# Weight splits tied to earlier products, and their loads issued from ScalarE's queue, in the attention stage of a decoder step

## The chip, the core and the metric

The kernel runs on one core of a Trainium2 chip. The core has five engines, each with a queue of its own that it works through in order: TensorE (PE in the profile; PEld is its weight load), VectorE (DVE), ScalarE (ACT), GpSimd (POOL) and SyncE (SP, which here only issues DMAs). A DMA is issued by an instruction in one of these queues and then moved by the core's 16 DMA engines. Time is the device time of one execution in microseconds (us). A measurement consists of several executions of each kernel on the same chip; their median is given.

## The reference

One layer of a gated decoder for 1024 prompt tokens and 64 sample tokens (8 sequences of 8), all in float32:

```
u = rmsnorm(x);  [a | q | k | v | g_a | g_b] = u @ w_in
A: causal pooling of a over windows 2/4/8/16, a linear map per group, @ w_pa
B: QK-normed dilated sliding-window attention, 3 groups of 4 heads,
   (window, dilation) = (128,1), (512,4), (2048,16); groups combined
   by their softmax denominators, @ w_pb
h = x + (sigmoid(g_a) * A + sigmoid(g_b) * B) @ w_o
y = h + relu(rmsnorm(h) @ w_up)^2 @ w_down
```

It also returns the new key/value windows and the last rows of the pooling input.

## The kernel before

Every float32 product is made of three products of rounded parts: each operand is split into a rounded high part and a low rest. For weights this is done by `split` (lines 92 to 95): ScalarE writes the rounded copy (line 93), VectorE writes the difference (line 94). Weights come as panels of 256 columns. `panel` (line 102) takes a panel in four pieces of 512 columns of its layout, each holding two of the eight 128-row blocks: `raw_piece` (line 97) loads a piece of 256 KB into one of three buffers `raw` (the DMA is line 99), and `split` writes it to one of three places in the tile `places`, which successive panels use in turn. A buffer takes its next load when both halves of its last split are done.

The kernel first makes the pooling input `a`, then the attention's q, k and v (this stage, about 60 to 408 us), then the gates and branches, the output projection, and the two large products of the feed-forward part, which take about half of the time.

The attention stage runs over the head groups in the order g = 2, 1, 0. Each group has three panels, q (j = 0), k (j = 1) and v (j = 2), which fill all three places. So a panel of the next group overwrites the panel of the same kind of the group before, and its pieces cannot be written before the last product with that panel is done. A group runs through blocks of 128 tokens: block 8 (the 64 sample tokens) together with block 0, then 1 to 5, then 6 and 7 together (one after the other in group 0). For a pair of blocks the products go q, q, k, k, v, v; for single blocks q and k are one product. `qkv_part` (line 522) issues one such product and records its last matmul in `ends_of[g, blk, j]`; the squares, the norms, the scales and the copies out of PSUM follow on ScalarE, VectorE and GpSimd. Between the products come the steps of attention of blocks that are ready (scores `sg`, transposes `tpg`, outputs `pog`), of the pooling branch and of the sample attention, which reads its cached keys and values (`pck`, `pcv`, `kts`, `vts`).

Only TensorE's order is written out by hand, in program order. All other queues are ordered by the framework's planner, which simulates the program, takes earlier instructions first among those it holds ready, and may pull a load far ahead of its place. `behind_pe` (line 124) adds a dependency of an instruction on a matmul, which holds it back in that plan and on the chip. In `panel`, the argument `after` gives one such matmul to the copy (line 93) of each of the four pieces. `load` (line 959) is the local function that makes a panel of a group with a list of such matmuls; group 2's three panels have none.

In the before, all loads of these panels are issued from SP's queue, as are nearly all other DMAs of the stage: the stores of keys and values (line 929), of attention outputs (lines 705 and 708), the reads of cached keys and values (lines 730, 798, 846), and the moves of small tiles. Only the first three pieces of the very first panel (`a0`) are issued from ScalarE's queue.

Of the kernel before, what the change touches and what calls it, by code (L numbers as in the profile page):

```python
# [32 lines left out]
def decoder_step(ctx, tc, i, o):  # L33
    nc = tc.nc
    v_, s_, g_, t_ = nc.vector, nc.scalar, nc.gpsimd, nc.tensor
    dma = nc.sync.dma_start
# [7 lines left out]
    def rr(p, shape, dt, name, tag, bufs):  # L44

        n = turn[p, tag] = turn.get((p, tag), -1) + 1
        return p.tile(shape, dt, name=name, tag=f"{tag}.{n % bufs}", bufs=1)
# [44 lines left out]
    def split(dst_hi, dst_lo, src):  # L92
        ins = s_.activation(dst_hi, src, AF.Copy)  # L93
        v_.tensor_tensor(dst_lo, src, dst_hi.bitcast(F32), op=ALU.subtract)  # L94
        return ins

    def raw_piece(src, name, a, load=dma):
        raw = rr(wp, [P, 512], F32, name=f"raw_{name}_{a}", tag="raw", bufs=3)
        load(raw, src[:, a:a + 512])
        return raw  # L100

    def panel(src, name, between=None, after=None, ahead=None):

        n = src.shape[1]
        wt = places[:, place[0] % 3]
        place[0] += 1
        for a in range(0, n, 512):
            raw = ahead.pop(0) if ahead else raw_piece(src, name, a)
            if between is not None:
                between(a // 512)  # L110
            ins = split(wt[:, 0, a:a + 512], wt[:, 1, a:a + 512], raw)
            if after is not None:
                behind_pe(ins, after[a // 512])
        throttle.append(ins)
        return wt
# [38 lines left out]
    def bank(name):  # L154
        held[0] = (held[0] + 1) % 4
        return acc_p.tile([P, 512], F32, name=name, tag=f"acc.{held[0]}", bufs=1)
# [238 lines left out]
    def flush():  # L395
        while later:
            later.pop(0)()
# [113 lines left out]
    ends_of = {}  # L511
# [10 lines left out]
    def qkv_part(g, wts, blk, name, tiles, js):  # L522


        n = min(P, TOK - blk * P)
        qk, vt = tiles
        go = 0 if blk == 8 else g
        pt = bank(f"p{''.join('qkv'[j] for j in js)}{name}")
        js = sorted(js, key=lambda j: wts[j])
        N = 256 * len(js)  # L530
        at = places[:, wts[js[0]]:wts[js[-1]] + 1:max(1, wts[js[-1]] - wts[js[0]])]

        def rhs(s, k):
            return at[:, :, s, k * 256:(k + 1) * 256]

        if blk == 8:
            for k in range(KD):
                t_.matmul(pt[:, :N], smp_t[:, k, :], rhs(0, k), start=(k == 0), stop=(k == KD - 1))
                if k < KD - 1:
                    for kk in ((0, 1) if k == 0 else (k + 1,)):  # L540
                        last_mm[0] = t_.matmul(pt[:n, :N], smp_t[:, kk, :NS], rhs(1, kk), start=False, stop=False)
            v_.tensor_copy(vt[:n], pt[n:, :256])
            v_.tensor_tensor(pt[:n, :256], pt[:n, :256], vt[:n], op=ALU.add)
        else:
            gemm(pt[:n, :N], KD, lambda s, k: block_cols(g, blk, s, k), rhs, g == 0, step if N > 256 else None)
        for j in js:
            ends_of[g, blk, j] = last_mm[0]
        if blk < 8:
            if g == 0 and 2 in js and blk < 7:
                in_order(blk + 1)  # L550
        if js[0] < 2:
            ms = rr(ap1, [P, 8], F32, name=f"ms{name}_{js[0]}", tag="ms", bufs=4)
            r = rr(ap1, [P, 8], F32, name=f"mr{name}_{js[0]}", tag="mr", bufs=4)
            H = 4 * len(js)
            for u, j in enumerate(js):
                for h in range(4):
                    s_.activation(qk[:n, j * 256 + h * HD:j * 256 + (h + 1) * HD],
                                  pt[:n, u * 256 + h * HD:u * 256 + (h + 1) * HD], AF.Square,
                                  accum_out=ms[:n, 4 * u + h:4 * u + h + 1])
            v_.tensor_scalar(ms[:n, :H], ms[:n, :H], 1.0 / HD, xeps[go][:n, blk:blk + 1], op0=ALU.mult, op1=ALU.add)  # L560
            g_.tensor_tensor(r[:n, :H], ms[:n, :H], mhalf[:n, :H], op=ALU.pow)  # L561

            def scale():
                for u, j in enumerate(js):
                    for h in range(4):
                        behind_pe(s_.activation(qk[:n, j * 256 + h * HD:j * 256 + (h + 1) * HD],
                                                pt[:n, u * 256 + h * HD:u * 256 + (h + 1) * HD], AF.Copy,
                                                scale=r[:n, 4 * u + h:4 * u + h + 1]))
                    if j and blk == 8:
                        v_.tensor_tensor(qk[:n, 256:], qk[:n, 256:], wrow[:n], op=ALU.mult)  # L570
        else:
            s_.activation(vt[:n], pt[:n, :256], AF.Copy, scale=rtok[go][:n, blk:blk + 1])
        step()
        if js[0] < 2:
            soon(scale)
# [356 lines left out]
    for g in (2, 1, 0):  # L932
        nq = i["qk_norm"]
        if g == 1:
            assert ("p", 3) in done
            flush()
            pa.close()
            pam.close()
            ap2 = pb2.enter_context(tc.tile_pool(name="att2", bufs=1, reuse_waits="tile"))
            sp1 = psm.enter_context(tc.tile_pool(name="smp1", bufs=1, side="right", reuse_waits="tile"))  # L940
            np_ = psm2.enter_context(tc.tile_pool(name="nat", bufs=1, side="right", reuse_waits="tile"))
            sp = psm2.enter_context(tc.tile_pool(name="smp2", bufs=1, side="right", reuse_waits="tile"))
            osm = ap2.tile([P, 3, 4, 66], F32, name="osm")

            for a in range(2):
                v_.memset(osm[64:, a], 0.0)
                v_.memset(osm[64:, a, :, 64], -NEG)
            qs = sp1.tile([P, 768], F32, name="qs")
            for hf in range(2):
                dma(qs[64 * hf:64 * hf + 64], new_d[2].rearrange("t b c -> (t b) c"))  # L950
            wq = sp1.tile([P, 2, 256], F32, name="wq", tag="ss")[:, 0]
            dma(wq, bass.AP(tensor=nq.tensor, offset=nq.offset + 2 * 512, ap=[[0, P], [1, 256]]))
            v_.scalar_tensor_tensor(qs[:, :256], wq, HD ** -0.5, qs[:, :256], op0=ALU.mult, op1=ALU.mult)
            own_keys = sample_own_keys(qs)
        wrow = ap1.tile([P, 256], F32, name=f"wrow{g}", tag="wrow")
        dma(wrow, bass.AP(tensor=nq.tensor, offset=nq.offset + g * 512 + 256, ap=[[0, P], [1, 256]]))
        wts = [(place[0] + j) % 3 for j in range(3)]

        def load(j, *after):
            panel(i["w_in"][2 + 3 * j + g], f"qkv{g}_{j}", after=[ends_of[a] for a in after] or None)  # L960


        if g == 2:
            load(0)
            load(1)
            load(2)
        else:
            h = g + 1
            load(0, (h, 6, 1), (h, 7, 1), (h, 6, 2), (h, 6, 2))
            load(1, (h, 6, 2), (h, 7, 2), (h, 7, 2), (h, 7, 2))  # L970
        for blks in ((8, 0), (1,), (2,), (3,), (4,), (5,)) + (((6, 7),) if g else ((6,), (7,))):
            if g == 1 and 6 in blks:
                in_order(0)
            tiles = {b: qkv_tiles(f"{g}_{b}", b == 8) for b in blks}

            for js in (((0, 1), (2,)) if blks[0] in (1, 2, 3, 4, 5) else ((0,), (1,), (2,))):
                for b in blks:
                    qkv_part(g, wts, b, f"{g}_{b}", tiles[b], js)
                    if g < 2 and b < 8:
                        own_step(1)  # L980
                    if 2 in js:
                        (sample_block if b == 8 else prompt_block)(g, b, *tiles[b])
                if g == 2 and 2 in js and 8 in blks:
                    start(pool_branch(), "p", now=True)
                if g < 2 and 0 in js and 8 in blks:
                    load(2, (g, 8, 0), (g, 0, 0), (g, 0, 0), (g, 0, 0))


    while (2, "own") not in done:
# [68 lines left out]
    for d in range(4):  # L1058
# [6 lines left out]
        ahead = gate("b", d, *units[0], wgb, 3) if d else sgb0[0]  # L1065
        for u, (c, m) in enumerate(units):
# [3 lines left out]
            name = f"{d}_{c}_{m}"  # L1070
            ga, gb = sga[u], ahead
            if u + 1 < len(units):
                ahead = gate("b", d, *units[u + 1], wgb, 3) if d or u > 1 else sgb0[u + 1]
# [73 lines left out]
    for d in range(4):  # L1147
# [5 lines left out]
        for c0, n in CHUNKS if d < 3 else [(r * R4, R4) for r in range(4)]:  # L1153
            for m in range(2):
# [3 lines left out]
                for q in range(4):  # L1158
                    a, b = max(c0, q * R4), min(c0 + n, (q + 1) * R4)
# [462 lines left out]
    for g, rows in ((2, 60), (1, 63), (0, 60)):  # L1622
        src, dst = i[f"cache_kv{g + 1}"], o[f"kv{g + 1}_sample"]
# [107 lines left out]
```

## Time and profile before

| | us |
|---|---|
| median of 3 executions (lowest, highest) | 1478.26 (1478.07, 1479.83) |
| the profiled execution | 1477.96 |
| its span in the trace | 1476.2 |
| mean granted TensorE clock | 0.989 of full speed |
| attention stage, 60 to 408 us: TensorE busy | 334.55 of 348 |

The span runs from the first to the last instruction in the trace; what is around it belongs to the execution's time too. In the profile's rows a group is named by line, engine, operation and tiles (out<-in), with its count; a row of waits gives who waited for whom, the total, the number of times and the longest, in us. A row of a timeline gives the start, the duration and what ran; what stands in brackets is the idle time of the engine before it and what ended it. In a row of windows stand the stretch, its length, the busy time of each engine with its number of instructions, the granted clock of TensorE as a share of full speed, the share of the DMA engines that was busy, and the rate at which they moved data.

### The profile page before, as it was taken

The page shows a single profiled execution, that of the slowest core. Times are in us where ns is not written, and L with a number is a line of the kernel's source. Part 1 is how long each engine was busy: PE and PEld are TensorE (multiplying, and loading weights), DVE is VectorE, ACT ScalarE, POOL GpSimd, SP SyncE. Part 2 cuts the span into 40 slices and gives each one's busy share as a digit, 9 for nine tenths or more (in the row PEclk, how much of TensorE's full clock was granted, in tenths as well). Part 3 has the DMA queues.
Part 4 walks back from the last instruction along what each step waited for, and adds up shares of the span by engine and source line. Part 5 has one row for each costly group of instructions (what it writes and reads, how often), then busy time and mean ns, then how long its engine had stood idle before and what let it go on. Part 6 is the DMA issues. An engine that isn't in the chain of part 4 may idle for free.

```text
span 1476.2 us, 28005 instructions
## 1 busy us (share of the span) xinstructions
PE 1445.6 (98%) x10595; PEld 1397.7 (95%) x10595; DVE 996.5 (68%) x1949; ACT 687.3 (47%) x1885; POOL 395.8 (27%) x619
## 2 busy tenths in 40 slices
PE   8999899989999999999999999999999999999998
PEld 8988788878999999999998999999998999999998
DVE  7565555667864443434668998888988567666686
ACT  8466745567784222222445656566556322222220
POOL 1611236645400000010200221221125534343330
PEclk9999899999999999999999999999999999999999
DMA  6311656865446557479620776766677889787642
GB/s 219 97 47 64 195 140 168 216 181 122 119 119 206 193 183 258 148 216 301 251 101 16 274 286 252 273 237 261 255 273 290 321 298 327 258 294 261 238 186 112
DMA packets 124277, 304.72 MB, mean 206 GB/s; under 512 B 19111, under 2 KB 72045, under 8 KB 118830
## 3 DMA queue, kind: packets, MB, share of 16 engines
q1 hardware_dynamic: 101182, 187.81, 38.9%
q0 software_dynamic: 22528, 114.34, 21.9%
q8 instruction: 83, 1.36, 0.4%
q10 hardware_dynamic: 432, 0.79, 0.2%
q14 instruction: 52, 0.43, 0.1%
HBM read 218.49 MB, written 128.05 MB: 235 GB/s over the span
## 4 chain that ended last, share of the span: by engine, by line
PE 87%; DMA 4%; DVE 3%; issue 3%; ACT 1%; POOL 1%; SPq 1%; ACTq 0%; DVEq 0%; POOLq 0%
PE p1d L1202 13%; PE p1u L1202 11%; PE pga L136 6%; PE pgb L136 6%; PE p2d L1202 6%; PE p2u L1202 6%; PE ph L136 6%; PE pqk L136 5%; PE pv L136 4%; PE a L264 3%; PE pa L136 3%; PE p3d L1202 3%; PE p3u L1202 3%; PE pb L136 2%; DMA raw_qkv<-in_w_in_dram 1%
## 5 line engine op out<-in xcount | busy, mean ns | idle before, releaser
L1202 PE MATMUL p1d<-act,places 128*128 128x272 f32 x1104 | 191.2, 288 | 1.8 <-DVE places L94 1.1
L1202 PEld LDWEIGHTS p1d<-act,places 128*128 128x128 f32 x1104 | 163.2, 188 | 2.7 <-DVE places L94 1.3
L1335 POOL DMA_DIRECT2D z_d<-zs_M x105 | 56.2, 535 | 245.7 <-DVE zs_M L94 242.5
L1582 DVE TENSOR_TENSOR yd<-yd,p1d 128x544 f32<-128x544 f32 x116 | 83.0, 716 | 39.9 <-PE p1d L1202 39.9
L1629 POOL DMA_DIRECT2D out_kv_sample_dram<-in_cache_kv_dram x44 | 22.3, 508 | 310.5 <-ACT places L93 294.8
L1202 PE MATMUL p1u<-t,places 128*128 128x272 f32 x768 | 103.0, 291 | 0.7 <-ACT q L1449 0.7
L1202 PE MATMUL p1u<-act,places 128*128 128x272 f32 x768 | 102.2, 289 | 1.3 <-ACT q L1377 1.3
L93 ACT ACTIVATE places<-sd 128x512 fp32r<-128x512 f32 x64 | 37.4, 625 | 140.0 <-issue 108.0
L1202 PEld LDWEIGHTS p1u<-t,places 128*128 128x128 f32 x768 | 99.7, 191 | 0.8 <-ACT q L1449 0.8
L1202 PEld LDWEIGHTS p1u<-act,places 128*128 128x128 f32 x768 | 98.6, 188 | 1.8 <-ACT q L1377 1.5
L136 PE MATMUL pga<-act,places 128*128 128x384 f32 (+1 forms) x576 | 98.0, 328 | 0.0
L136 PE MATMUL pgb<-act,places 128*128 128x384 f32 (+1 forms) x576 | 97.8, 326 | 0.0
L1202 PE MATMUL p2d<-act,places 128*128 128x272 f32 x528 | 94.0, 288 | 1.6 <-DVE places L94 1.0
L136 PE MATMUL ph<-act,places 128*128 128x384 f32 (+2 forms) x624 | 95.4, 314 | 0.0
L136 PEld LDWEIGHTS pgb<-act,places 128*128 128x128 f32 x576 | 95.3, 188 | 0.0
L136 PEld LDWEIGHTS ph<-act,places 128*128 128x128 f32 x624 | 95.3, 188 | 0.0
L136 PEld LDWEIGHTS pga<-act,places 128*128 128x128 f32 x576 | 94.6, 188 | 0.3
L93 ACT ACTIVATE places<-rd 128x512 fp32r<-128x512 f32 x64 | 37.1, 625 | 94.7 <-PE p1d L1202 94.7
L1202 PEld LDWEIGHTS p2d<-act,places 128*128 128x128 f32 x528 | 78.9, 188 | 2.3 <-DVE places L94 1.2
L561 POOL TENSOR_TENSOR mr<-ms,mhalf 128x4 f32<-128x4 f32 (+2 forms) x39 | 49.7, 1273 | 112.9 <-DVE ms L560 107.4
L1534 POOL TENSOR_TENSOR sd<-rd 128x128 f32<-128x128 f32 x64 | 38.0, 594 | 118.6 <-DVE places L94 103.6
L94 DVE TENSOR_TENSOR zs_M<-q,zs_M 128x544 fp32r<-128x544 f32 x75 | 54.0, 722 | 18.8 <-ACT zs_M L93 18.8
(383 smaller groups left out, 3646.8 us busy)
## 6 DMA issues: line engine op xcount, KB each, us to landing
z_d<-zs_M POOLq DMA_DIRECT2D x105, 544.0 KB, 4.9
act<-z_d SPq DMA_DIRECT2D x73, 544.0 KB
out_kv_sample_dram<-in_cache_kv_dram POOLq DMA_DIRECT2D x36, 960.0 KB, 7.3
ru<-in_w_up_dram SPq DMA_DIRECT2D x16, 1024.0 KB
rd<-in_w_down_dram SPq DMA_DIRECT2D x15, 1024.0 KB
raw_qkv<-in_w_in_dram SPq DMA_DIRECT2D x36, 256.0 KB
zc<-z_d SPq DMA_DIRECT2D x16, 544.0 KB
pck<-in_cache_kv_dram SPq DMA_DIRECT2D x32, 256.0 KB
```

Of the source, the lines that this page charges most:

```text
L93: ins = s_.activation(dst_hi, src, AF.Copy)
L94: v_.tensor_tensor(dst_lo, src, dst_hi.bitcast(F32), op=ALU.subtract)
L136: last_mm[0] = t_.matmul(out, lhs(a, k), rhs(b, k), start=(j == 0), stop=(j == len(terms) - 1))
L264: last_mm[0] = t_.matmul(pts[m][:, :n], wt[:, a, kk, m * P:(m + 1) * P], act4[b][kk][:, :, part4(c)], start=(p == 0 and kk == 0), stop=(p ...
L561: g_.tensor_tensor(r[:n, :H], ms[:n, :H], mhalf[:n, :H], op=ALU.pow)
L1202: last_mm[0] = t_.matmul(pt[:, s, :R4], w(a, k), z(b, k, s), start=(start and j == 0), stop=(j == len(terms) - 1), skip_group_check=True)
L1335: g_.dma_start(z_d[f][AT[m]], st.rearrange("p b l -> p (b l)").bitcast(F32))
L1534: ins = g_.tensor_tensor(s[:, 0], a21, a22, op=ALU.add)
L1582: v_.tensor_tensor(part, part, p[src], op=ALU.add)
L1629: ins = g_.dma_start(d, a)
```

## The change

It has three parts, all for the panels of groups 1 and 0; group 2's stay as they are.

First, `panel` takes the issuing engine as an argument, and the 24 loads of groups 1 and 0 are issued from ScalarE's queue in place of SP's.

Second, the copies are tied to earlier products. Written as (product's block and kind), for the next group's pieces 1 to 4, with 6q for block 6 of the group before and s for the sample block of the group itself:

| panel | before | after |
|---|---|---|
| q | 6k, 7k, 6v, 6v | 7q, 6k, 6k, 7k |
| k | 6v, 7v, 7v, 7v | 7k, 6v, 6v, 7v |
| v | s q, 0q, 0q, 0q | 7v, s q, s q, s q |

Third, the v panel is made in the program one step earlier: right behind the sample's q product, where it stood behind block 0's q product.

```diff
-    def panel(src, name, between=None, after=None, ahead=None):
+    def panel(src, name, between=None, after=None, ahead=None, load=dma):
...
-            raw = ahead.pop(0) if ahead else raw_piece(src, name, a)
+            raw = ahead.pop(0) if ahead else raw_piece(src, name, a, load)
...
         def load(j, *after):
-            panel(i["w_in"][2 + 3 * j + g], f"qkv{g}_{j}", after=[ends_of[a] for a in after] or None)
+            panel(i["w_in"][2 + 3 * j + g], f"qkv{g}_{j}", after=[ends_of[a] for a in after] or None,
+                  load=nc.scalar.dma_start if after else dma)
...
-            load(0, (h, 6, 1), (h, 7, 1), (h, 6, 2), (h, 6, 2))
-            load(1, (h, 6, 2), (h, 7, 2), (h, 7, 2), (h, 7, 2))
+            load(0, (h, 7, 0), (h, 6, 1), (h, 6, 1), (h, 7, 1))
+            load(1, (h, 7, 1), (h, 6, 2), (h, 6, 2), (h, 7, 2))
...
                     qkv_part(g, wts, b, f"{g}_{b}", tiles[b], js)
+                    if g < 2 and b == 8 and 0 in js:
+                        load(2, (g + 1, 7, 2), (g, 8, 0), (g, 8, 0), (g, 8, 0))
...
-                if g < 2 and 0 in js and 8 in blks:
-                    load(2, (g, 8, 0), (g, 0, 0), (g, 0, 0), (g, 0, 0))
```

## The prediction, before the changed kernel was timed

> **What bounds it now.** First the page's head: the span, and how much of it TensorE (PE) works.
>
> ```profile
> span 1476.2 us, 28005 instructions
> PE 1445.6 (98%) x10595; PEld 1397.7 (95%) x10595; DVE 996.5 (68%) x1949; ACT 687.3 (47%) x1885; POOL 395.8 (27%) x619
> ```
>
> PE is the bound, 98% busy, so an edit of loads and waits can only win PE's pauses and the slow matmuls behind them. The waits of PE from 60 to 410 us, all attention, say who ends its pauses (total, times, longest):
>
> ```profile
> PE pv L541 <- DVE places L94: 4.9, 4, 3.1
> PE sg1b L597 <- ACT ocg1b L631: 2.5, 1, 2.5
> PE pq L541 <- DVE places L94: 2.0, 2, 1.3
> PE pv L538 <- ACT places L93: 1.9, 1, 1.9
> PE tps L828 <- DVE pxs L822: 0.9, 1, 0.9
> ```
>
> Three of the five name `places`, the split weights that the change is about. They sit at the two group changes: the v panel of group 1 (174 to 184 us), the q panel of group 0 (282 to 285 us). A pause costs more than itself. The windows just behind these pauses (length, PE busy, PEld, DVE, ACT, POOL, granted clock, DMA share, GB/s):
>
> ```profile
> 176.00:190.00 14.00, 9.13 (x42) 7.63 (x42) 5.84 (x19) 9.22 (x48) 3.93 (x5) 0.51 0.60 165
> 284.00:290.00 6.00, 5.40 (x43) 4.84 (x44) 3.80 (x8) 2.18 (x4) 2.82 (x4) 0.72 1.01 270
> 298.00:304.00 6.00, 5.08 (x30) 4.85 (x31) 4.26 (x17) 5.18 (x29) 1.53 (x3) 0.72 0.98 274
> ```
>
> The clock fell to 0.51, 0.72, 0.72 of full speed. Busy time at clock c loses (1 - c) of itself, so three places have a price:
>
> - A, group 1's v: pauses 1.9 + 4.9 = 6.8, plus 9.13 x 0.49 = 4.5: **11.3 us**.
> - B, group 0's q: pauses 2.0, plus 5.40 x 0.28 = 1.5: **3.5 us**.
> - C, the attention step sg1b: pause 2.5, plus 5.08 x 0.28 = 1.4: **3.9 us**.
>
> Together 18.7, with the 0.9 of tps 19.6 us: the most that the change can win.
>
> The Trainium skill, page "TensorE: Matmul & The Clock Gate", section "Part 1: The HAM clock gate", has the clock halved after an idle window of about 3.4 us. The floor of one half agrees with the 0.51; the pauses here are shorter each (3.1 us the longest) and still cost, so the rows decide. With the pauses alone the three places would hold 11.3 us, not 18.7.
>
> **Why A happens.** A piece of weights is loaded into one of three buffers, copied by ScalarE (ACT, L93), and the rest is subtracted by VectorE (DVE, L94); then the buffer takes the piece three places later. Group 1's first v piece follows the second k piece. Timelines of DVE, SP's queue and ACT:
>
> ```profile
> 162.91 0.69 DVE L94 TENSOR_TENSOR places<-raw_qkv,places 128x512 fp32r<-128x512 f32 x1
> ```
> ```profile
> 163.70 0.43 SPq L929 DMA_DIRECT2D out_kv_prompt_dram<-kw  x1
> 164.18 0.85 SPq L929 DMA_DIRECT2D out_kv_prompt_dram<-v  x1
> 165.07 1.12 SPq L950 DMA_DIRECT2D qs<-new_d  x2
> 166.28 0.53 SPq L952 DMA_DIRECT2D wq<-in_qk_norm_dram  x1
> 166.86 0.43 SPq L956 DMA_DIRECT2D wrow<-in_qk_norm_dram  x1
> 167.33 2.56 SPq L730 DMA_DIRECT2D pck<-in_cache_kv_dram  x2
> 169.99 2.41 SPq L99 DMA_DIRECT2D raw_qkv<-in_w_in_dram  x3
> ```
> ```profile
> 175.00 0.63 ACT L93 ACTIVATE places<-raw_qkv 128x512 fp32r<-128x512 f32 x1 [3.37 <-DMA raw_qkv<-in_w_in_dram]
> ```
>
> The buffer was free at 162.91 + 0.69 = 163.60; SP issued the load at 169.99, 6.4 us later, behind eight other DMAs; ACT had the data at 175.00 and a copy at 175.63, when PE had paused 1.9 us for it: PE wanted it from 173.7. The wait that ends last is thus SP's order, and then the transfer.
>
> **The ties.** The products that hold back the copies (b0 = block 0):
>
> ```profile
> 145.20 3.13 PE L136 MATMUL pk<-places,act 128*128 128x256 f32 x24
> 152.87 3.17 PE L136 MATMUL pv<-places,act 128*128 128x256 f32 x24
> 157.13 3.34 PE L136 MATMUL pv<-places,act 128*128 128x256 f32 x24
> 163.68 3.11 PE L136 MATMUL pq<-places,act 128*128 128x256 f32 x24
> ```
>
> They end at 148.3 (block 6's k), 156.0 and 160.5 (blocks 6's and 7's v), 166.8 (b0's q). The first copy moves from 148.3 to block 7's q, a product earlier. The second k piece, whose buffer the first v piece needs, moves from 160.5 to 156.0. The last three v pieces no longer wait for 166.8, but for the sample's q, done by 163.7.
>
> New chain at A: one load took 3.58 to 5.87 us from issue to landing (two rows of the chain of work), and ACT came to its first copy 1.9 us after its tie of 148.3:
>
> ```profile
> 158.65 3.58 DMA raw_qkv<-in_w_in_dram
> 176.76 5.87 DMA raw_qkv<-in_w_in_dram
> ```
> ```profile
> 150.22 0.70 ACT L93 ACTIVATE places<-raw_qkv 128x512 fp32r<-128x512 f32 x1
> ```
>
> The second k piece can be copied from 156.0. With 1.9 us for ACT to come to it and 0.63 + 0.69 for its two halves, its buffer is free at about 159.3 (an estimate). The first v load, issued then from ACT, lands at 163 to 166 and is split by 166.5 to 169; the fourth v piece, which takes that buffer, is ready at 171.5 to 176.5. PE wants the first at 173.7 and the fourth up to 2.4 us later (three quarters of the at most 3.2 us, 160.5 to 163.7, that the sample's q took). So A goes whole or but for about 1 us; I take **-11.3**.
>
> B: PE and ACT around group 0's q.
>
> ```profile
> 264.68 2.97 PE L136 MATMUL pk<-places,act 128*128 128x256 f32 x24
> 273.07 2.99 PE L136 MATMUL pv<-places,act 128*128 128x256 f32 x24
> 280.77 0.36 PE L538 MATMUL pq<-places,smp_t 128*128 128x256 f32 x1
> 280.17 1.14 ACT L93 ACTIVATE places<-raw_qkv 128x512 fp32r<-128x512 f32 x2
> 282.51 0.68 DVE L94 TENSOR_TENSOR places<-raw_qkv,places 128x512 fp32r<-128x512 f32 x1
> ```
>
> The third q piece was tied to 276.1 and ready at 283.2, after the product had begun at 280.8. Its new tie is 267.7; with the same lag of 7.1 us it is ready at 274.8. **-3.5.**
>
> C: ACT waits in its own order for a transfer, and what PE needs stands behind it:
>
> ```profile
> 297.98 0.63 ACT L93 ACTIVATE places<-raw_qkv 128x512 fp32r<-128x512 f32 x1 [1.49 <-DMA raw_qkv<-in_w_in_dram]
> 298.52 0.35 ACT L631 COPY ocg1b<-pog1b 128x256 f32<-128x256 f32 x1
> ```
>
> The v loads come some us earlier, but copies tied less are held by their data alone, so ACT may meet such a wait elsewhere. I take half: **-2.0** (bounds 0 and -3.9).
>
> **What it costs.** 24 loads go through ACT. The only loads issued there in the before, and the waits of SP for the subtract ahead of a load (140 to 192 us, then 260 to 304):
>
> ```profile
> L99 ACTq DMA_DIRECT2D raw_a<-in_w_in_dram x3: 413/450/453, 0.7 to 1.7; - x3
> ```
> ```profile
> SPq L99 <- DVE places L94: 9.7, 6, 3.3
> ```
> ```profile
> SPq L99 <- DVE places L94: 5.8, 6, 1.7
> ```
>
> Issuing: 24 x 0.45 = 10.8 us of ACT, hidden while ACT is not the bound; it is busy 36.09 of 52 and 30.07 of 50 us there:
>
> ```profile
> 140.00:192.00 52.00, 45.23 (x336) 41.81 (x336) 26.71 (x88) 36.09 (x167) 11.98 (x14) 0.87 0.55 159
> 260.00:310.00 50.00, 44.61 (x399) 41.31 (x398) 37.27 (x99) 30.07 (x140) 28.91 (x37) 0.93 0.72 197
> ```
>
> Waiting is dearer. A load in ACT's order holds everything behind it until DVE has done the subtract: the squares and scales of q and k, the softmax exponentials, the copies out of PSUM, and for these PE waits. No row shows such a wait on ACT. Its bounds are 0 (ACT is sent to the load only when the buffer is free) and the 9.7 + 5.8 = 15.5 us that SP stood; passed to PE with its slow clock (C: 3.9 for 2.5, a factor 1.56) that is 24.2. Nearest is C itself, the one time that ACT's order stopped PE: I take one more such stall, **+3.9**. SP loses 24 issues; no PE wait above names a load that this brings forward, so 0, at most the 0.9 of tps.
>
> **Sum.** -11.3 - 3.5 - 2.0 + 3.9 = -12.9. The profiled execution took 1477.96 us (span 1476.2 and 1.8 around it), 0.3 under the median of 1478.26, so I use it as it is: 1477.96 - 12.9 = **1465 us**.
>
> **Rivals.**
>
> *Loads on ACT stall PE (slower).* Place: ACT's order at both group changes, above all the second, where DVE's subtract came late (copied from 280.17, subtracted at 282.51). A and B are won (14.8), C stays, and all of the 15.5 is passed on: -14.8 + 24.2 = +9.4, 1487 us. It decides from 14.8 / 1.56 = 9.5 us of the 15.5 on. For it: C. Against: PE waited for ACT just once in 350 us but for the split itself.
>
> *The transfers are the limit.* The share of the DMA engines before and during the critical loads:
>
> ```profile
> 150.00:162.00 12.00, 12.00 (x99) 11.39 (x98) 6.38 (x21) 9.44 (x37) 1.73 (x2) 1.00 0.43 115
> 162.00:174.00 12.00, 11.78 (x101) 11.28 (x99) 7.04 (x21) 8.57 (x35) 1.68 (x2) 1.00 0.89 268
> ```
>
> At 0.89 an earlier load may only share the same engines. Then half of A is won (5.6) and B (3.5), C stays and the new stall comes: 1477.96 - 9.1 + 3.9 = 1473 us. Against: 0.43 just before, where the loads now move.
>
> The Trainium skill, "DMA: Bandwidth & Descriptors", section "Issuing engines are not separate DMA queues", speaks for this rival: all queues share the same engines, and another issuing engine saves only sequencer time, "usually small relative to the DMA itself". Here the 6.4 us on SP was more than the 5.0 of the transfer, so the trace does not bear out "small" at A.
>
> *It does not do what it says.* All engines but PE are ordered by the framework's planner. If it puts the v loads behind long work on ACT, A only changes its name: about 1478.
>
> **Chances.** Forecast 0.55, transfers 0.16, no effect 0.13, slower 0.15, better than all named 0.01. A measurement of this kernel tells about 0.2%, 3 us, from no change: faster 0.72, same 0.13, slower 0.15. The forecast's own range is 1459 to 1470. Range: down to 1477.96 - 19.6 = 1458, up to 1480, which takes in the transfers and no effect and leaves out the slower case.
>
> **What would show it.** Right: PE's waits for `places` gone or under 1 us in all; clock 1.00 through both group changes; 24 `raw_qkv` loads in ACT's queue, the first v load of group 1 issued by about 160. Wrong: new PE waits that end on ACT's squares, scales or exponentials, with ACT idle ahead of its own L99; or the v copies still waiting over 3 us for their data.

## The result, and the profile after

The changed kernel took 1469.27 us in the median of six executions (1465.20 to 1473.39), the kernel before 1478.74 (1477.85 to 1479.83, six executions, same chip): a ratio of 0.9937, 95% interval 0.9925 to 0.9949, or 9.5 us less. The forecast was 1465. One execution of a later run (e8), of 2707.62 us at a clock of 0.91, is left out of that run's median below, which would be 1469.98 with it.

The profiled execution of the changed kernel took 1469.14 us, its span 1467.4. The head of its page and PE's waits from 60 to 410 us (who waited for whom, total, times, longest):

```profile
span 1467.4 us, 27992 instructions
PE 1441.1 (98%) x10595; PEld 1393.8 (95%) x10595; DVE 996.6 (68%) x1949; ACT 687.2 (47%) x1885; POOL 399.9 (27%) x619
```
```profile
PE pss L813 <- issue: 2.5, 1, 2.5
PE sg1b L597 <- ACT ocg1b L631: 2.0, 1, 2.0
PE pos L855 <- DMA vts<-in_cache_kv_dram: 1.7, 1, 1.7
PE pv L541 <- DVE places L94: 1.0, 1, 1.0
```

The pauses for `places` fell from 8.8 us to 1.0. Three others stand above them now: `pss`, the scores of the sample attention, which before waited only once, 0.5 us for a transfer at another place; `sg1b`, which was there with 2.5; and `pos`, with 0.8 before.

Where the time went is read from windows laid at about the same places of the work in both kernels: group 1's v product of the sample, the rest of group 1, the change to group 0, the rest of the attention. First before, then after (stretch, length, PE busy, PEld, DVE, ACT, POOL, granted clock, DMA share, GB/s):

```profile
174.00:192.00 18.00, 11.46 (x56) 9.69 (x57) 8.33 (x30) 10.97 (x52) 6.27 (x9) 0.62 0.57 155
192.00:280.80 88.80, 88.30 (x723) 75.45 (x721) 52.41 (x150) 49.67 (x257) 54.34 (x69) 1.00 0.70 172
280.80:300.00 19.20, 14.73 (x127) 13.01 (x125) 14.55 (x37) 11.25 (x42) 7.54 (x10) 0.89 0.88 241
300.00:408.80 108.80, 107.08 (x833) 92.36 (x833) 81.09 (x254) 80.22 (x351) 55.19 (x68) 0.99 0.56 141
```
```profile
174.00:182.00 8.00, 6.61 (x54) 5.81 (x53) 5.23 (x28) 6.81 (x39) 4.46 (x7) 1.00 1.17 215
182.00:271.50 89.50, 89.35 (x723) 76.18 (x724) 54.30 (x154) 52.28 (x266) 53.54 (x68) 1.00 0.73 178
271.50:290.00 18.50, 13.85 (x124) 12.45 (x124) 14.03 (x34) 11.29 (x42) 9.11 (x12) 0.90 0.81 223
290.00:399.20 109.20, 107.50 (x839) 92.94 (x837) 80.86 (x255) 80.82 (x356) 58.33 (x68) 0.99 0.57 141
```

The lengths say where: 18.0 to 8.0 at group 1's v, with the clock back from 0.62 to 1.00; then 88.8 to 89.5, 19.2 to 18.5, 108.8 to 109.2; and behind 408.8 and 399.2 the rest of the span is 1067.4 and 1068.2. So 10.0 us were won at one place, A, and 1.2 net were lost elsewhere in small pieces. The change to group 0, where B and C were to bring 5.5, brought 0.7, and 0.4 of it was lost again right behind it.

At A the chain of loads runs as the ties let it. Two rows of the chain of waits of after (start, us), the loads of the second and third v piece, and three of ACT's timeline, the issue of the first v load and the copies of the first and the fourth piece:

```profile
161.66 4.50 DMA raw_qkv<-in_w_in_dram
166.25 5.10 DMA raw_qkv<-in_w_in_dram
```
```profile
159.58 0.34 ACTq L99 DMA_DIRECT2D raw_qkv<-in_w_in_dram  x1
164.12 0.64 ACT L93 ACTIVATE places<-raw_qkv 128x512 fp32r<-128x512 f32 x1
173.99 0.65 ACT L93 ACTIVATE places<-raw_qkv 128x512 fp32r<-128x512 f32 x1
```

The first v load is issued at 159.58 (before: 169.99), the first piece is copied at 164.12 (before: 175.00), and PE loses 1.0 us, to the fourth piece, whose subtract stands behind other work of DVE and ends at 176.83.

At B the q product of group 0 no longer waits for its weights, but what follows it does. PE's, DVE's and POOL's timelines of after, and, in the last two fences, `pss` and the copies that it needs as they ran in the kernel before:

```profile
271.53 0.36 PE L538 MATMUL pq<-places,smp_t 128*128 128x256 f32 x1
276.16 1.13 PE L813 MATMUL pss<-kts,qSs 128*32 128x136 f32 x16 [2.51 <-issue]
```
```profile
272.79 1.22 DVE L746 TENSOR_REDUCE sc<-pck 128x16 f32<-128x1024 f32 x1 [1.32 <-POOL pck L744]
275.72 0.72 DVE L807 COPY qSs<-qkn 64x8 f32<-64x8 f32 x4
```
```profile
269.21 3.54 POOL L744 TENSOR_TENSOR pck<-pck,qs 128x256 f32<-128x256 f32 x4 [1.30 <-DMA pck<-in_cache_kv_dram]
```
```profile
285.22 0.99 PE L813 MATMUL pss<-kts,qSs 128*32 128x136 f32 x16
```
```profile
283.11 0.71 DVE L807 COPY qSs<-qkn 64x8 f32<-64x8 f32 x4
```

`pss` needs the four copies of the sample's queries (line 807). They stand in DVE's order behind a reduce of the sample's own keys (line 746), which waits for POOL, and POOL waits for the transfer of `pck`. In the changed kernel `pss` starts 276.16 - 275.72 = 0.44 us behind the start of its copies. By that it could have started at 283.11 + 0.44 = 283.55 before, where PE, held up at the q weights, came to it only at 285.22: B's pause hid this one, and without it at most 1.7 us were to be won (an estimate from these rows).

Not even that is seen at this place, because the copies also came later behind the start of group 0's q product: 275.72 - 271.53 = 4.19 us in place of 283.11 - 280.77 = 2.34. PE had moved forward by 9.2 us, the reduce of line 746 only from 280.19 to 272.79, 7.4 us. So PE stands 2.51 us ahead of `pss`, the clock behind it is 0.50 for two us, and B's price comes back under another name. The same pause stands in e4 (2.8 us), where group 0 alone is changed; why POOL's work comes later was not separated.

### The profile page after: what moved, and what is told of

Read it like the earlier page. It is cut to its first block, busy times and chain, and to the rows that moved or that the text cites. A ratio compares the mean times of both kernels' runs of the same rounds, so it can differ in the third digit from the quotient of the medians.

```text
span 1467.4 us, 27992 instructions
## 1 busy us (share of the span) xinstructions
PE 1441.1 (98%) x10595; PEld 1393.8 (95%) x10595; DVE 996.6 (68%) x1949; ACT 687.2 (47%) x1885; POOL 399.9 (27%) x619
## 4 chain that ended last, share of the span: by engine, by line
PE 77%; issue 9%; DMA 5%; DVE 4%; POOL 2%; ACT 2%; SPq 0%; POOLq 0%; ACTq 0%; DVEq 0%
PE p1d L1203 13%; PE ph L136 6%; PE pgb L136 6%; PE p2d L1203 6%; PE p1u L1203 6%; PE pqk L136 6%; PE pga L136 5%; PE pv L136 4%; PE a L264 3%; PE pa L136 3%; PE p3d L1203 3%; PE p2u L1203 3%; DMA raw_qkv<-in_w_in_dram 2%; PE pb L136 2%; POOL z_d L1336 2%
```

## The experiments

Each of e1 to e12 was timed against the kernel before on the same chip; the chip was not the same for all of them, so they are compared by their ratios. "Pause at A" is PE's waits for `places` from 172 to 194 us of the profiled execution, group 1's v.

| run | what differs | median, us | ratio (95%) | pause at A |
|---|---|---|---|---|
| the kernel before | median by measurement | 1478.26 to 1478.95 | 1 | 6.8 |
| the change | | 1469.27 | 0.9937 (0.9925 to 0.9949) | 1.0 |
| e1_ties_only | from after: loads on SP | 1467.28 | 0.9915 (0.9894 to 0.9937) | 0.5 |
| e2_queue_only | from before: loads on ACT | 1477.15 | 0.9985 (0.9972 to 0.9998) | 9.0 |
| e3_group1_only | the whole change, group 1 alone | 1468.72 | 0.9926 (0.9906 to 0.9946) | 1.0 |
| e4_group0_only | the whole change, group 0 alone | 1477.73 | 0.9985 (0.9970 to 1.0001) | 9.2 |
| e5_qk_ties_sp | q and k ties, loads on SP | 1469.32 | 0.9934 (0.9912 to 0.9957) | 2.4 |
| e6_v_ties_sp | v ties and place, loads on SP | 1478.95 | 1.0005 (0.9991 to 1.0018) | 7.9 |
| e7_group1_sp | group 1's ties, loads on SP | 1467.66 | 0.9927 (0.9907 to 0.9947) | none |
| e8_late_reduce | e1, with line 746's last reduce later | 1469.4 | 0.9930 (0.9908 to 0.9952) | not read |
| e9_after_late_reduce | after, with the same edit | 1472.82 | 0.9954 (0.9940 to 0.9967) | 0.9 |
| e10_q_ties_g1 | before, group 1's q ties | 1479.43 | 1.0001 (0.9990 to 1.0011) | 7.4 |
| e11_queue_late_qs | e2, with line 953 later | 1477.58 | 0.9992 (0.9981 to 1.0003) | 9.0 |
| e12_two_ties | before, two ties of group 1 | 1474.46 | 0.9977 (0.9967 to 0.9988) | 4.4 |

### The parts of the change

First the two halves, ties and queue, each alone. e1 is the changed kernel with

```diff
-                  load=nc.scalar.dma_start if after else dma)
+                  load=dma)
```

> The new ties and the earlier place of the v panel, with all loads on SP as before. Queue theory (A was SP's order): the first v load still stands behind the stores and cached keys on SP, so most of A's 11.3 us stays and the time is 1474 to 1479. Tie theory (A was the late release of the buffers): the loads move forward in SP's order by themselves, A goes, 1467 to 1471, like the changed kernel.

e2 is the kernel before with only the first two hunks of the change (the issuing engine), at the old ties and the old place of the v panel.

> The 24 loads on ScalarE, with the old ties and the old place of the v panel. Queue theory: the pause before group 1's sample v product falls from 6.8 us to under 2 and the time is 1467 to 1471. Tie theory: the v copies wait for block 0's q and the buffers come free as late as before, so A keeps at least half: 1473 to 1479.

The ties alone bring everything, 1467.28 us; the queue alone at most 0.3%, 1477.15. SP's queue in e1 shows why it can stay: the planner, given buffers that come free sooner, puts the first v loads ahead of the stores by itself (start, time taken, count).

```profile
153.77 8.61 SPq L99 DMA_DIRECT2D raw_qkv<-in_w_in_dram  x6
162.60 0.34 SPq L929 DMA_DIRECT2D out_kv_prompt_dram<-kw  x1
168.86 0.85 SPq L99 DMA_DIRECT2D raw_qkv<-in_w_in_dram  x2
```

And e2's timelines of ACT and DVE show what stops the loads when only the queue is freed:

```profile
167.09 0.34 ACTq L99 DMA_DIRECT2D raw_qkv<-in_w_in_dram  x1
172.94 0.63 ACT L93 ACTIVATE places<-raw_qkv 128x512 fp32r<-128x512 f32 x1 [0.76 <-DMA raw_qkv<-in_w_in_dram]
```
```profile
174.78 0.42 DVE L953 SCALAR_TENSOR_TENSOR qs<-wq,qs 128x256 f32<-128x256 f32 x1 [3.87 <-DMA wq<-in_qk_norm_dram]
177.54 0.68 DVE L94 TENSOR_TENSOR places<-raw_qkv,places 128x512 fp32r<-128x512 f32 x1
186.43 0.69 DVE L94 TENSOR_TENSOR places<-raw_qkv,places 128x512 fp32r<-128x512 f32 x1 [5.61 <-ACT places L93]
```

This profile runs 1.5 us later than that of before already ahead of A (block 0's q product starts at 165.22 against 163.68), so the times are counted from that start. The first v load goes 4.4 us sooner than in the before (167.09 - 165.22 = 1.87 against 169.99 - 163.68 = 6.31) and its piece is copied 3.6 us sooner, but its subtract then stands on DVE behind the product of line 953, which waits 3.87 us for `wq`. The fourth piece takes that buffer, and its subtract comes 1.6 us later than in the before (186.43 and 183.31, less the starts).

The same question by group:

```diff
-            load(0, (h, 7, 0), (h, 6, 1), (h, 6, 1), (h, 7, 1))
-            load(1, (h, 7, 1), (h, 6, 2), (h, 6, 2), (h, 7, 2))
+            if g == 1:
+                load(0, (h, 7, 0), (h, 6, 1), (h, 6, 1), (h, 7, 1))
+                load(1, (h, 7, 1), (h, 6, 2), (h, 6, 2), (h, 7, 2))
+            else:
+                load(0, (h, 6, 1), (h, 7, 1), (h, 6, 2), (h, 6, 2))
+                load(1, (h, 6, 2), (h, 7, 2), (h, 7, 2), (h, 7, 2))
```

with the v panel and the issuing engine by group in the same way; e4 has `g == 0` there.

> The whole change for group 1 alone; group 0 as before. Theory that the second group change hides another wait behind the weights: 1469, like the changed kernel (within 1.5 us), with PE again pausing some 2 us for group 0's q pieces. Rival (both group changes pay): group 0's part is missing, 1471 to 1473.

> The whole change for group 0 alone; group 1 as before. Theory of the hidden wait: no gain, 1477 to 1480, with the pause at group 0's q replaced by one before the scores of the sample attention. Rival (B is won, as predicted): 1473 to 1475.

e3 keeps the whole gain, 1468.72 us, and e4 almost none, 1477.73. e4's time alone would not settle it: in its profile the pauses at A are longer than in the kernel before (9.2 us against 6.8), and group 0's q product starts 2.7 us later, so a gain of that size behind it would not show. But e3, without group 0's part, is as fast as the change. So all of the gain that can be seen is won at group 1. e7 then takes e3 and puts its loads back on SP:

> All three panels of group 1 alone are tied as in the changed kernel, group 0 is as before, and every load stays on SP's queue. Theory (all that was won lies at group 1, and by the ties): 1466 to 1470 us, as the kernel with group 1 changed and its loads on ScalarE (1468.72). Rival (with group 0 as before, the loads of group 1 on ScalarE carried part of it): 1471 to 1475 us.

1467.66 us: group 1's ties are the change. Its PE waits from 60 to 410 us begin with the one that the kernel before had at B, left in place at no cost that can be seen. The window behind these two pauses shows one reason: the clock stays at 1.00, where it was 0.72 over six us in the kernel before:

```profile
PE pq L541 <- DVE places L94: 2.0, 2, 1.4
```
```profile
276.00:282.00 6.00, 5.71 (x60) 5.22 (x57) 2.94 (x7) 2.15 (x4) 2.85 (x4) 1.00 1.05 275
```

### Which ties

e5 is e1 with the v panels back at their old ties and place, e6 is e1 with the q and k panels back at theirs:

```diff
-                    if g < 2 and b == 8 and 0 in js:
-                        load(2, (g + 1, 7, 2), (g, 8, 0), (g, 8, 0), (g, 8, 0))
...
+                if g < 2 and 0 in js and 8 in blks:
+                    load(2, (g, 8, 0), (g, 0, 0), (g, 0, 0), (g, 0, 0))
```

> Only the q and k panels take the new ties; the v panels keep their old ties and their old place in the program, and all loads stay on SP's queue. Theory 1 (what won A is that the second k piece is copied sooner, so that its buffer, the one that the first v piece needs, comes free sooner): the old v ties end at 166.8, seven us ahead of the time at which PE wants v, so they bind little; nearly all is kept, 1467 to 1471 us, and PE's pauses for places in group 1's v stay under 1.5 us. Theory 2 (what won A is that the v panel stands earlier in the program and is tied less, so that its loads and subtracts go ahead of the stores, the qs product and the other work of that moment): 1474 to 1479 us, and the pauses for places are 4 us or more.

> Only the v panels are tied as in the changed kernel and made at their earlier place; the q and k panels keep their old ties, and all loads stay on SP's queue. Theory 1: the second k piece is still tied to 160.5 and its buffer is still free only at 163.6; B's ties are the old ones; half of A at most: 1472 to 1477 us. Theory 2: the v loads are issued right at 163.6, ahead of the stores, and land by 169, in time for 173.7; the q product of group 0 pauses as before, but that was worth nothing: 1467 to 1471 us.

Theory 1 is borne out in both: 1469.32 with the q and k ties, 1478.95 with the v ties, where not even the half of A came that it allowed for (1472 to 1477). In e5 the pauses for `places` are 2.4 us, over the 1.5 expected, so the v ties are worth one or two microseconds of pause, which its time does not resolve. In e6 the stall stands at its old place. The load of the fourth v piece, from the chain of waits, and that piece's subtract on DVE:

```profile
176.94 6.38 DMA raw_qkv<-in_w_in_dram
```
```profile
184.00 0.69 DVE L94 TENSOR_TENSOR places<-raw_qkv,places 128x512 fp32r<-128x512 f32 x1 [3.21 <-ACT places L93]
```

PE stands 6.9 of e6's 7.9 us for this one piece, whose load could not start before the first v piece had been split; and the first v load itself was issued at 168.26, 3.7 us after its buffer was free, behind the stores on SP. In three buffers the piece n takes the buffer of piece n - 3, so four pieces form a chain: third q, second k, first v, fourth v. In the before the load of the second k piece started at 158.65 and took 3.58 us (the row in the prediction), so it was there at 162.23, after its tie of 160.5: to move it, its load must move, and that waits for the third q piece. Two runs test this. e10 moves group 1's q ties alone, in the kernel before; e12 moves two ties alone, one in q and one in k:

```diff
-            load(0, (h, 6, 1), (h, 7, 1), (h, 6, 2), (h, 6, 2))
-            load(1, (h, 6, 2), (h, 7, 2), (h, 7, 2), (h, 7, 2))
+            load(0, (h, 6, 1), (h, 7, 1), (h, 6, 1) if g == 1 else (h, 6, 2), (h, 6, 2))
+            load(1, (h, 6, 2), (h, 6, 2) if g == 1 else (h, 7, 2), (h, 7, 2), (h, 7, 2))
```

> The kernel before with one line edited: the q panel of group 1 alone takes its new ties; k, v, all of group 0 and the queue of all loads are as before. It frees the loads of k earlier, but the second k piece keeps its tie of 160.5. Theory (the first v piece waits for the second k piece's buffer, so q and k must both move): the first v load is still issued behind the stores at 168 to 170, A stays, 1476 to 1480 us. Rival (any earlier split of group 1 lets the chain of loads run ahead): 1468 to 1473 us.

> The kernel before with two of its ties moved, both in group 1: the third q piece from block 6's v product to block 6's k, and the second k piece from block 7's v to block 6's v. Everything else, the queue of the loads included, is as before. Theory (A is a chain through one buffer: third q piece, second k piece, first v piece, fourth v piece, each load waiting for the split before it): these two ties free the whole chain; PE's pauses for places in group 1's v fall from 6.8 us to under 2, and the time is 1467 to 1471 us, nearly all that the whole change brings. Rival (it takes the ties of the whole panels, since the other two buffers are late as well): 1473 to 1479 us.

e10 gives nothing (1479.43), as the chain says: the second k piece kept its tie. e12 gives 0.9977, 3.9 us of the ten. Its 1474.46 us and its pauses of 4.4 us lie on the rival's side (1473 to 1479, not under 2): the chain through this one buffer is a part of A, and the pieces in the other two buffers are late as well. The ACT, DVE and SP rows of e12:

```profile
162.82 0.63 ACT L93 ACTIVATE places<-raw_qkv 128x512 fp32r<-128x512 f32 x1 [0.85 <-DMA raw_qkv<-in_w_in_dram]
176.96 0.63 ACT L93 ACTIVATE places<-raw_qkv 128x512 fp32r<-128x512 f32 x1 [4.74 <-DMA raw_qkv<-in_w_in_dram]
```
```profile
163.73 0.70 DVE L94 TENSOR_TENSOR places<-raw_qkv,places 128x512 fp32r<-128x512 f32 x1
```
```profile
168.33 1.34 SPq L730 DMA_DIRECT2D pck<-in_cache_kv_dram  x2
169.77 1.50 SPq L99 DMA_DIRECT2D raw_qkv<-in_w_in_dram  x3
```

With the first v piece early, the second is the late one. Its buffer, that of the third k piece, is free at 163.73 + 0.70 = 164.43, its load is issued at 169.77, 5.3 us later, behind stores and `pck`, takes 7.17 us, and is copied at 176.96; PE's longest pause is 3.8 us for it. Issued when the buffer was free, it would have been there at 171.6, ahead of PE's pause, which begins at 175.1 (an estimate from these rows). So here SP's order is what is waited for. The same two ties with the loads on ACT were not run.

### The queue, with VectorE out of its way

e11 is e2 with line 953 moved into the own keys' steps and held behind block 0's k product:

```diff
-            v_.scalar_tensor_tensor(qs[:, :256], wq, HD ** -0.5, qs[:, :256], op0=ALU.mult, op1=ALU.mult)
...
         loaded = [piece(0, 0, "k0")]
         yield
+        behind_pe(v_.scalar_tensor_tensor(qs[:, :256], wq, HD ** -0.5, qs[:, :256], op0=ALU.mult, op1=ALU.mult))
```

> The kernel with only the queue moved (loads on ScalarE, old ties, 1477.15 us), and the product that forms qs put behind block 0's k product, so that the subtract of the first v piece no longer stands behind it on VectorE while it waits for the transfer of wq. Nothing is left out. Theory A (with the queue and VectorE's order both out of the way, the loads on ScalarE do win A): the first v piece is split by 175, the fourth by 181, 1470 to 1473 us. Theory B (the buffers come free too late for any queue: the first v load cannot be issued before 163.6 to 167 and the fourth only once the first is split, then 4 to 6 us of transfer): the first pause of v falls from 3 to under 1 us, but one of 3 us or more for the fourth piece stays, 1474 to 1477 us.

Theory B's side, though 0.6 us above its range: 1477.58 us. Its rows of DVE, ACT and PE:

```profile
172.81 0.69 DVE L94 TENSOR_TENSOR places<-raw_qkv,places 128x512 fp32r<-128x512 f32 x1
```
```profile
177.14 0.33 ACTq L99 DMA_DIRECT2D raw_qkv<-in_w_in_dram  x1
183.56 0.63 ACT L93 ACTIVATE places<-raw_qkv 128x512 fp32r<-128x512 f32 x1 [4.13 <-DMA raw_qkv<-in_w_in_dram]
```
```profile
184.97 0.47 PE L541 MATMUL pv<-places,smp_t 128*64 128x256 f32 x1 [7.91 <-DVE places L94]
```

The first v piece is now split at 173.50, in time, and PE's first pause falls to 1.1 us. But the fourth piece's load, free to start at 173.50, is issued at 177.14: ACT stands in copies, scales, squares and exponentials of its own for 3.6 us, and its order holds the load just as SP's did. The subtract of the fourth piece starts at 184.22 all the same, and the pause merely moved: 7.9 us ahead of that piece. Without the 3.6 us in ACT's order, 4.3 of them would still have stood (an estimate), so the buffer did come free too late.

### What hid behind B

e8 and e9 take away the wait that `pss` met, in e1 and in the changed kernel: two steps of the own keys are left out behind blocks 6 and 7 of group 1 (the steps come later), so that the last reduce of line 746 stands behind the query copies.

```diff
-                    if g < 2 and b < 8:
+                    if g < 2 and b < 8 and not (g == 1 and b in (6, 7) and 2 in js):
                         own_step(1)
```

> The kernel with all new ties and all loads on SP (1467.28 us), with one more edit: the last reduce of the sample's own keys, which waits for POOL and stands in VectorE's order ahead of the query copies that pss needs, is put two steps later in the program, behind these copies. Nothing is left out. Theory (group 0's earlier q only uncovered the wait of pss, and that wait ends on VectorE's order): the pause of pss of 1.8 us goes, and the slow clock behind it: 1463 to 1465.5 us. Rival (a third wait stands right behind, for the kts transfers or for the copies of weights that now go into the same moment): 1466.5 to 1469 us, with another name in PE's waits between 270 and 290 us.

> The changed kernel itself (loads on ScalarE, all new ties) with the last reduce of the sample's own keys two steps later in the program, behind the query copies that pss needs. Nothing is left out. Theory (B's gain was taken by the wait of pss, which ends on VectorE's order): pss pauses under 0.5 us where it paused 2.5, the clock stays near 1.00 up to the next pause, and from the start of the sample's q product to the start of the next attention outputs it takes 7 us or less in place of 10.5; the time is then 1465 to 1467 us. Rival (the next wait comes right behind, as the same edit on the kernel with its loads on SP gave 1469.98 against 1467.28): pss no longer pauses, but another wait of 2 us or more stands within the next 15 us, and the time stays at 1468 to 1471 us.

e8 took 1467.40 to 1470.11 us, no better than e1; no profile of it is shown. e9 took 1472.82, above the change's 1469.27, with intervals of the ratios that overlap. Its PE waits from 60 to 410 us and the window at the change to group 0:

```profile
PE tps L827 <- ACT ps L817: 1.6, 1, 1.6
PE pss L813 <- DMA kts<-in_kT_dram: 1.5, 2, 1.0
PE tcg0b L720 <- DVE ocg0b L654: 1.1, 1, 1.1
PE pog1b L628 <- ACT pTg1b L619: 1.1, 1, 1.1
```
```profile
272.60:290.00 17.40, 14.49 (x140) 13.06 (x139) 12.65 (x33) 11.58 (x46) 3.12 (x4) 1.00 0.77 232
```

DVE's order no longer stops `pss`, and the clock stays at 1.00; but now the transfer of `kts` does, for 1.0 us (the other 0.5 stands at 209 us), and behind it come waits for copies and for the softmax's exponentials, none of them over 1.6 us. The rival has the mechanism, other waits right behind; the time is above even its range (1468 to 1471). One number sums up group 0: from the start of its sample's q product to the first gate product (line 136, `pga`; count, shortest/median/longest ns, first and last start; in the order before, after, and e9 behind the start of its q product)

```profile
L136 PE MATMUL pga<-act,places x576: 303/334/443, 408.8 to 640.7; 128*128 128x384 f32 x128, 128*128 128x320 f32 x64
```
```profile
L136 PE MATMUL pga<-act,places x576: 302/334/442, 399.2 to 632.4; 128*128 128x384 f32 x128, 128*128 128x320 f32 x64
```
```profile
272.56 0.36 PE L538 MATMUL pq<-places,smp_t 128*128 128x256 f32 x1
```
```profile
L136 PE MATMUL pga<-act,places x576: 302/334/442, 400.6 to 638.6; 128*128 128x384 f32 x128, 128*128 128x320 f32 x64
```

it takes 408.8 - 280.77 = 128.0 us before, 399.2 - 271.53 = 127.7 after, and 400.6 - 272.56 = 128.0 in e9. The pauses change their names, and the stretch keeps its length in these three. In the other profiles, one execution each, it is 126.0 to 126.8 with group 0's new q and k ties (e1, e4, e5) and 127.9 to 130.2 with its old ones (the other seven), so these ties may well win a microsecond or two here. With both groups changed, what is won does not arrive: among the gates behind it the last attention steps of group 0 still run, and from the first to the last start of `pga` it takes 640.7 - 408.8 = 231.9 us before, but 632.4 - 399.2 = 233.2 after, 233.3 in e5, 234.6 in e1 and 638.6 - 400.6 = 238.0 in e9 (an execution of 1475.22 us, the longest of its five); in e4 it is 231.8. What sets these lengths, among POOL, the transfers and DVE, was not separated.

## Why the prediction was right, and where its steps were not

**A, -11.3: right in place and nearly in size.** It brought 10.0. The times worked out for the new chain were close: the first v load at about 159.3 (159.58), landing at 163 to 166 (copied at 164.12), the fourth piece ready at 171.5 to 176.5 (its subtract ended at 176.8), about 1 us left (1.0).

**The step of A that failed is the one from its cause to the queue**: "The wait that ends last is thus SP's order, and then the transfer." The 6.4 us between the free buffer and the issue were read off SP's queue rightly, but they were one of several things in a row. PE's longest pause, 3.1 us, was for the fourth v piece, the last in a chain of loads through one buffer, and that load did not stand in SP's order: the subtract of the first v piece ended at 175.66 + 0.99 = 176.65 in the kernel before, and the load started at 176.76.

```profile
175.66 0.99 DVE L94 TENSOR_TENSOR places<-raw_qkv,places 128x512 fp32r<-128x512 f32 x1 [0.21 <-ACT places L93]
```

With the loads off SP alone (e2, e11) the time is within 0.3% of before, since the orders of DVE (e2) and ACT (e11) delay the same chain, and with the loads left on SP and the ties moved (e1, e7) the whole gain is there. The working for the new ties followed the chain and so came out right although the sentence on the cause did not.

That SP's order has no part in A is not shown. It holds a v load for 6.4 us in the kernel before, 3.7 in e6 and 5.3 in e12, and the ties also work by letting the planner put loads ahead of the stores (e1). Had the first v load gone at 163.60, the same steps would have had the fourth v piece split 6.4 us earlier, at 177.6 in place of 184.0, where PE would want it at about 176 (an estimate from the rows of before). Neither the old ties with a queue that stands idle nor the v ties with the loads on ACT was run.

**B, -3.5: nothing that the times show.** The 2.0 us at the weights went, as forecast, but the step didn't ask what was late next. `pss` was: it could have started 1.7 us ahead of its start in the kernel before, as a row of DVE said, and in the changed kernel its operands came 1.85 us later still behind the q product. Nor is the slow clock, 1.5 of the 3.5, a fixed price: behind two pauses of 2.0 us in all the clock was 0.72 before and 1.00 in e7. In e3 and e7 B stays and nothing is lost that can be seen.

**C, -2.0: about -0.2.** `sg1b` waits 2.0 us as against 2.5, again for `ocg1b`, and ACT stands again at a copy of weights for a transfer just ahead of it. From the first outputs behind group 0's q products (`pog1b`) to the start of its sample's v product it took 304.05 - 291.19 = 12.86 us before and 294.69 - 282.00 = 12.69 after. Taking half, for want of a row, was too much.

**The new stall on ACT, +3.9: not there.** The one new wait of PE in the stage that ends on ACT's work is of 0.3 us (`pqk`, on the scales). The 24 issues took 0.33 to 0.59 us each, most 0.33, less than the 0.45 taken. What the runs show is the reverse of the fear: in e11 it is not the load that holds up ACT's work but ACT's work that holds up the load, by 3.6 us. Of the signs named for being right, one did not come: the clock fell to 0.50 behind `pss` at the change to group 0.

**The sum** was -12.9 and came out at -8.8 in the profiled spans: 1.3 too much at A, 3.5 at B, 1.8 at C, against the 3.9 that was not paid, and 1.4 lost in small pieces (the 1.2 net above, without C's 0.2), among them a new pause of 1.3 us for the last attention step of group 0 in the gates (`tcg0b`). That pause, or a like one, shows in the profiles with the new ties in both groups, not in those of e3, e4 and e7; e2, with the old ties, has one of 1.8. That the sum comes as near as it does is partly luck: a stall that did not come makes up for most of what B and C did not bring.

**The rivals.** The slower one (loads on ACT stall PE) is out. The transfers did not set the limit at A: the two v loads took 4.50 and 5.10 us, and the DMA share was 1.17, the highest of the windows shown, in the very one that ran at full clock. The rule of the Trainium skill, page "DMA: Bandwidth & Descriptors", section "Issuing engines are not separate DMA queues", by which another issuing engine saves only a little sequencer time, was held in the prediction not to be borne out at A. e2's ratio of 0.9985 agrees with it. But e2 does not show the wait in SP's queue to be small: the first v load did go 4.4 us sooner, counted from block 0's q product, and this was lost again in DVE's order.

Whether the queue does good or harm once the ties are moved stays open: 0.9937 with it and 0.9915 without (0.9926 and 0.9927 for group 1 alone), with intervals that overlap. The simplest kernel, e7, is as fast as any here; none is measurably faster than the change.

## What to carry to other kernels

When a load is late, follow its buffer back through the loads that held it before, not only the queue that issues it: with three buffers a late split comes back three pieces later, and the first piece of that chain which can be freed is where to begin; here the ties of the other two buffers were needed as well. Before a pause is priced, look up when the operands of the next instructions on the same engine were ready; if that is within the pause, only the difference can be won. Try the parts of a change alone: here the ties of one group carried all of the gain that can be seen.

## What the runs showed of the hardware

A pause of 2.51 us ahead of `pss` was followed by a clock of 0.50:

```profile
276.00:278.00 2.00, 1.84 (x20) 1.32 (x21) 1.93 (x6) 0.79 (x2) 0.31 (x1) 0.50 1.12 240
```

Shorter pauses at this place cost clock in one run and not in another. In the kernel before two pauses of 2.0 us in all (the longest 1.3) were followed by 0.72 over six us, in e7 two pauses of 2.0 us in all (the longest 1.4) by 1.00. So the length of a pause alone does not tell here whether the clock falls; what else decides is not shown.

The Trainium skill, page "TensorE: Matmul & The Clock Gate", section "Part 1: The HAM clock gate", gives an idle window of about 3.4 us ahead of the half clock. The pauses here were shorter, and some of them cost clock.
